# A decoder trunk on one core: attention scores of two pairs in one TensorE group, value products of two pairs together, inverse roots spread by transposes, and a table of holding times in the planner

## The chip, the cores and the metric

The kernel runs on one core of a Trainium2 chip. The metric is device time in microseconds (us) of one execution; three runs of the kernel before gave 423.72, 424.61 and 425.31 us, so the median is 424.61 us. The engines are called as the profile calls them: PE (TensorE's matmuls), PEld (its weight loads, which overlap the matmuls), DVE (VectorE), ACT (ScalarE), POOL (GpSimd) and SP (SyncE, which issues the loads).

## The reference

The program is a two-layer decoder trunk over 256 positions of width 1024. Layer 0 has three head groups that all read one normalized input: sparse attention with three branches (8 query heads in 2 key-value groups), block attention (8 heads) and cross-attention into 256 memory tokens (4 heads). Layer 1 has a retention group and the memory cross-attention again. Each group has a SiLU gate path; the gated outputs go through one output projection and are added to the residual. Cut to what the change touches:

```python
# sparse attention: branches c (compressed blocks), s (selected blocks), w (window)
o_s = einsum(masked_softmax(einsum(q, k_sel) * scale, causal), v_sel)
o_w = einsum(masked_softmax(einsum(q, k_win) * scale, causal), v_win)
o   = gate[0] * o_c + gate[1] * o_s + gate[2] * o_w

# block attention: with 256 positions only the causal own block is left
o = einsum(masked_softmax(einsum(q, k_own) * scale, causal), v_own)

# memory cross-attention, in both layers
o = einsum(softmax(einsum(q, k_mem) * scale), v_mem)

# rms_norm, on x, on the memory and between the layers
y = x * rsqrt(mean(x * x) + eps) * g
```

With 256 positions there are four blocks of 64 to select from and 16 may be taken, so that the selected branch is causal attention over all positions, as the window branch is.

## The kernel before

All activations lie with 256 tokens as two tiles of 128 rows, or turned, with 128 channels in the partitions. A weight arrives as f32 in a `raw` buffer (6 of them), is split into a rounded part `whi` (a cast on ACT) and a rest `wlo` (a subtraction on DVE), with four buffers of each, and three fp32r products (high times high, low times high, high times low) make up one projection in the PSUM banks `bpj`. These projections fill most of PE's time. Between them stand short pieces of plain fp32 work on PE, called groups here, which belong together and aren't interrupted:

- **Score groups** (`pair_scores`, `side_by_side`). Two heads of 64 channels form a pair: one head's operands are in partitions 0 to 63 and the other's in 64 to 127, and their products alternate. They appear in the trace as matmuls of form 64\*128 into the two banks `bs`. A causal pair needs four products (two of 128 columns, two of 256), a memory pair four of 256; the trace has two matmuls for each product.
- **Value groups** (`causal_values`, `mem_attention`). The two heads' outputs go to the two halves of the bank `bo`, in form 128\*64.
- **Transposes** of the weights `p` between softmax and value product, three or four at a time into the one bank `bt`. ACT copies that bank to a `pt` buffer before the next group of transposes may write it. The transposes of rotated queries and keys go to the one bank `btr`.
- **Spreading** (`spread`): three times a column of inverse roots is needed along the free axis; a plain fp32 matmul of the column, broadcast over 128 columns, with the identity does that, into `btr`.

There are eight PSUM banks: three `bpj`, two `bs`, and one each of `btr`, `bt` and `bo`. A pair's softmax is `causal_weights`: DVE adds the mask and takes the maximum, ACT takes the exponential with its sum, DVE the reciprocal, and the scaling is divided between them.

The order on each engine is not that of the code. The class `Plan` records every operation with an estimated price (`price`) and dependencies, and plays a schedule forward (`once`): at each step the engine whose next operation can start first takes it. On PE a group (kind 1: transposes and other plain products, kind 2: score form, kind 3: value form) is not taken the moment its inputs are there, while PE is on fp32r projections (kind 0): it waits until its inputs have been there for `HOLD` = 2000 ns, for every group alike (`order`). `turn` is the estimated price of going from one kind to another, and `arrange` plays 12 rounds with due times from the round before and keeps the best. The order so found is fixed in the program; the engines wait for one another by semaphores. The loads on SP and the order of POOL keep the order of the code.

In the code of layer 0 the sparse pairs 0 to 3 are done one by one (`sparse_pair`), each with a score group for each of two branches and one value group for both; then the memory group with a score and a value group for each of its two pairs; then the block pairs 0 to 3 one by one. In layer 1 the memory group has two score groups and one value group.

Of the kernel before, what the change touches and what calls it, by code (L numbers as in the profile page):

```python
# [16 lines left out]
P = 128  # L17
T = 256
# [31 lines left out]
class Op:  # L50
    __slots__ = ("lane", "calls", "cost", "left", "next", "at", "rank", "kind", "end", "held", "strict", "t", "due", "goal", "spent")


ROUNDS = 12
SLACK = 250
HOLD = 2000
FETCH = 6000
LEAD = 0
RELAX = 3000


class Plan:
# [74 lines left out]
    def add(self, lane, method, args, kw):  # L137
# [29 lines left out]
        step = self.price(lane, method, args, kw, out, reads)  # L167
        op.cost += step
        return op

    def price(self, lane, method, args, kw, out, reads):
        n = out.free_size()
        psum = any(a.tensor.name in self.psum for a in reads)
        if lane == "PE":
            if method == "transpose":
                return 110
            rhs, lhs = args[2], args[1]
            if rhs.dtype == F32R:
                return n / 2.4 + 14
# [44 lines left out]

    def turn(self, mode, kind):
        if mode == kind:
            return 0
        return 95 * (mode > 1 or kind > 1) + (150 if mode > 1 else 50) * (kind == 0)

    def arrange(self):  # L230
        ops = self.ops
        last = {}
        for op in ops:
            op.kind = self.mode(op) if op.lane == "PE" else 0
            op.due = op.rank
            for d in op.left:
                d.next.append((op, True))
            if op.strict or op.lane == "SP":
                if op.lane in last:
                    last[op.lane].next.append((op, False))  # L240
                    op.left.add(("after", last[op.lane]))
                last[op.lane] = op
        best = None
# [29 lines left out]
    def once(self):  # L273
# [8 lines left out]
        while len(done) < len(ops):  # L282
# [22 lines left out]
            if any(c[0] == "dma_start" for c in op.calls):  # L305
# [3 lines left out]
                op.end = dma[0] + 500  # L309
# [11 lines left out]
    def order(self, op, l, now, s, mode):  # L321
        early = max(s, now)
        if l == "PE":
# [6 lines left out]
            return ((0 if s + HOLD < now else 2) if op.kind else 1, 0, op.rank)  # L330
# [10 lines left out]
def trunk(  # L341
# [388 lines left out]
    read = []  # L730

    def pair_scores(q, k, spans):

        s = [bank("s") for _ in range(2)]
        side_by_side([(s[hh][:, a], q[pair_half(hh), tok * P : tok * P + P], k[pair_half(hh), : a.stop - a.start], True, True)
                      for tok, a in enumerate(spans) for hh in range(2)], *read)
        read.clear()
        return [[s[hh][:, a] for a in spans] for hh in range(2)], s

    def causal_weights(ss, gate):  # L740
# [11 lines left out]
        pt = tl("pt", [P, 2, 512], 2)  # L752
# [24 lines left out]
    def mem_attention(eqT, kT, v, szT, y, together):  # L777
        for pr in range(2):
            if pr == 0 or not together:
                o = bank("o")  # L780
                todo, done = [], []
# [4 lines left out]
            _, ss = pair_scores(eqT[:, pr], kT[:, pr], WHOLE)  # L786
# [8 lines left out]
            for hh in range(2):  # L795
                V.reciprocal(sm[:, hh], sm[:, hh])
                for tok in range(2):
# [3 lines left out]
                    else:  # L801
# [3 lines left out]
            c = slice(pr * T, (pr + 1) * T) if together else slice(0, T)  # L805
            todo += [(o[hh * 64 : hh * 64 + 64, c], v[:, kt, (2 * pr + hh) * 64 : (2 * pr + hh + 1) * 64],
                      pt[:, hh, kt * T : (kt + 1) * T], kt == 0 and c.start == 0, kt == 1, *[1] * together) for kt in range(2) for hh in range(2)]
            done.append(got)
            if pr == 0 and together:
                continue  # L810
            side_by_side(todo, *done)
            for i in range(0 if together else pr, pr + 1):
                gated(o[:, i * T : (i + 1) * T] if together else o, szT[:, i], y, i)
# [113 lines left out]
    def sparse_pair(pr):  # L927
        nonlocal kS, vsw, nq, gates, vcR, pcT
        o = bank("o")
        for half in vcR:  # L930
            PE.matmul(o[:, :T], half[:, pr % 2].rearrange("p g f -> p (g f)"), pcT[:, pr // 2], start=half is vcR[0], stop=False)
        todo, done = [], []
        for br in (1, 2):
            pt, got = causal_weights(pair_scores(nq[:, pr], kS[:, br - 1], SPAN)[0],
                                     gates[:, :, br * 8 + 2 * pr : br * 8 + 2 * pr + 2])
            todo += causal_values(pt, lambda g, kt, br=br: vsw[:, kt, (br - 1) * P + g * 64 : (br - 1) * P + g * 64 + 64],
                                  o, False, br == 2)
            done.append(got)
        side_by_side(todo, *done)
        gated(o, szn[:, pr], yn, pr)  # L940
# [47 lines left out]
    def memory_group():  # L988
        nonlocal eqS, szm, memk, memv
        mem_attention(eqS, memk, memv, szm, ym, False)  # L990
# [22 lines left out]
    def block_pairs(*prs):  # L1013
# [6 lines left out]
        for i, pr in enumerate(prs):  # L1020
            pt, got = causal_weights(pair_scores(mq[:, pr], mk[:, pr], SPAN)[0], None)
# [15 lines left out]
    for pr in range(4):  # L1037
        sparse_pair(pr)
# [6 lines left out]
    block_pairs(0)  # L1045
    block_pairs(1)
    block_pairs(2)
    block_pairs(3)

# [87 lines left out]
    mem_attention(eqS1, k1m, v1m, szm1, ym1, True)  # L1137
# [236 lines left out]
```

## Time and profile before

| what | value |
|---|---|
| three runs | 423.72, 424.61, 425.31 us (median 424.61) |
| span of the profiled execution, first to last instruction | 421.8 us; the runs' median is 2.8 us above it |
| PE busy | 415.1 us, 98% of the span, 2320 matmuls |
| DVE busy | 316.4 us, 75% |
| ACT busy | 259.0 us, 61% |
| POOL busy | 10.2 us, 2% |
| granted TensorE clock, mean | 0.998 |
| DMA | 74.20 MB, 176 GB/s on average |

In the timeline a row gives the start and the length of one or more equal instructions in a stretch, both in us, and their count. PE's matmuls are pipelined: the length of one runs into the next, so that what an instruction costs PE is read from start to start. In the view of waits a row says who waited for whom: the total in us, the number of times and the longest. In the view by windows each engine's busy time in a stretch stands beside the number of its instructions. Nearly all operations are recorded by one helper line (337), so that the names of the tiles tell them apart.

### The profile page before, as it was taken

The page shows a single profiled execution, that of the slowest core. Times are in us where ns is not written, and L with a number is a line of the kernel's source. Part 1 is how long each engine was busy: PE and PEld are TensorE (multiplying, and loading weights), DVE is VectorE, ACT ScalarE, POOL GpSimd, SP SyncE. Part 2 cuts the span into 40 slices and gives each one's busy share as a digit, 9 for nine tenths or more (in the row PEclk, how much of TensorE's full clock was granted, in tenths as well). Part 3 has the DMA queues.
Part 4 walks back from the last instruction along what each step waited for, and adds up shares of the span by engine and source line. Part 5 has one row for each costly group of instructions (what it writes and reads, how often), then busy time and mean ns, then how long its engine had stood idle before and what let it go on. Part 6 is the DMA issues. An engine that isn't in the chain of part 4 may idle for free.

```text
span 421.8 us, 6467 instructions
## 1 busy us (share of the span) xinstructions
PE 415.1 (98%) x2320; PEld 344.6 (82%) x2320; DVE 316.4 (75%) x643; ACT 259.0 (61%) x487; POOL 10.2 (2%) x23
## 2 busy tenths in 40 slices
PE   9999999999999999999999999999999999999994
PEld 8988988778878767778887878888888888888884
DVE  3889999999985658647788985865997486564634
ACT  4866648998767558645566745655655455654512
POOL 0000000000000000000000000100100010010001
PEclk9999999999999999999999999999999999999999
DMA  7998844457343392341685544555455555545302
GB/s 228 399 338 265 279 162 141 149 175 253 125 131 120 99 344 76 131 149 50 203 250 197 167 153 149 169 176 194 142 198 180 177 170 172 177 148 186 117 0 99
DMA packets 36975, 74.20 MB, mean 176 GB/s; under 512 B 3024, under 2 KB 22736, under 8 KB 36944
## 3 DMA queue, kind: packets, MB, share of 16 engines
q1 hardware_dynamic: 36512, 73.27, 52.9%
q10 hardware_dynamic: 432, 0.52, 0.4%
q8 instruction: 18, 0.29, 0.3%
q14 instruction: 13, 0.11, 0.1%
HBM read 72.74 MB, written 1.05 MB: 175 GB/s over the span
## 4 chain that ended last, share of the span: by engine, by line
PE 98%; DVE 0%; ACT 0%; issue 0%; POOL 0%; POOLq 0%
PE bpj L337 74%; PE bs L337 10%; PE btr L337 6%; PE bt L337 5%; PE bo L337 4%; ACT p L337 0%; DVE p L337 0%; DVE v L337 0%; DVE rot_b L337 0%; POOL p L337 0%; DVE ss L337 0%; POOL mhalf L337 0%; POOLq L1363 0%
## 5 line engine op out<-in xcount | busy, mean ns | idle before, releaser
L337 DVE TENSOR_TENSOR wlo<-raw,whi 128x1024 fp32r<-128x1024 f32 (+3 forms) x127 | 147.0, 1165 | 56.5 <-ACT whi L337 55.5
L337 ACT CAST whi<-raw 128x1024 fp32r<-128x1024 f32 (+3 forms) x127 | 127.0, 1004 | 80.7 <-PE bpj L337 43.0
L337 PE MATMUL bpj<-whi,big 128*128 128x512 f32 (+1 forms) x496 | 156.0, 387 | 0.0
L337 PEld LDWEIGHTS bpj<-whi,big 128*128 128x128 f32 x496 | 91.8, 188 | 18.7 <-issue 1.3
L337 PE MATMUL bpj<-wlo,big 128*128 128x512 f32 (+1 forms) x248 | 95.8, 386 | 0.0
L337 PE MATMUL bpj<-big,whi 128*128 128x512 f32 (+1 forms) x320 | 79.2, 377 | 0.0
L337 PEld LDWEIGHTS bpj<-big,whi 128*128 128x128 f32 x320 | 53.6, 192 | 7.6 <-issue 0.4
L337 PEld LDWEIGHTS bpj<-wlo,big 128*128 128x128 f32 x248 | 46.6, 188 | 8.8 <-issue 0.3
L337 PE MATMUL bpj<-big,wlo 128*128 128x256 f32 x288 | 46.1, 286 | 0.0
L337 PEld LDWEIGHTS bpj<-big,wlo 128*128 128x128 f32 x288 | 42.2, 190 | 4.7 <-issue 0.7
L337 PE MATMUL bpj<-whi,y 128*128 128x512 f32 x84 | 28.2, 392 | 0.0
L337 ACT COPY pt<-bt 128x384 f32<-128x384 f32 (+1 forms) x32 | 16.2, 505 | 10.3 <-PE bt L337 10.2
L337 ACT ACTIVATE p<-p,mx 128x128 f32<-128x128 f32 (+1 forms) x48 | 21.4, 450 | 1.6 <-DVE mx L337 1.6
L337 PEld LDWEIGHTS bpj<-whi,y 128*128 128x128 f32 x84 | 15.7, 188 | 3.1
L337 ACT COPY rot_a<-bpj 128x256 f32<-128x256 f32 x32 | 11.8, 368 | 9.5 <-PE bpj L337 9.3
L337 PE MATMUL bt<-cst,p 128*128 128x128 f32 x104 | 17.1, 277 | 0.0
L337 PE MATMUL bpj<-wlo,y 128*128 128x512 f32 x42 | 16.6, 396 | 0.0
L337 PEld LDWEIGHTS bt<-cst,p 128*128 128x128 f32 x104 | 12.3, 140 | 4.9 <-issue 2.6
L337 DVE CUSTOM_DVE_ANT_0 p<-bs,cst 128x128 f32<-128x128 f32 (+1 forms) x48 | 14.5, 353 | 1.0 <-PE bs L337 0.8
L337 DVE TENSOR_SCALAR p<-p,sm 128x256 f32<-128x256 f32 (+1 forms) x48 | 14.2, 323 | 1.2
L337 DVE TENSOR_TENSOR rot_a<-bpj,rot_a 128x256 f32<-128x256 f32 x32 | 13.4, 419 | 2.2 <-ACT rot_a L337 2.1
L337 ACT ACTIVATE v<-bpj,rstd 128x512 f32<-128x512 f32 (+1 forms) x18 | 12.4, 689 | 4.0 <-PE bpj L337 2.7
(227 smaller groups left out, 489.7 us busy)
## 6 DMA issues: line engine op xcount, KB each, us to landing
raw<-in_w SPq DMA_DIRECT2D x84, 512.0 KB, 4.4
raw<-in_wout SPq DMA_DIRECT2D x28, 512.0 KB, 3.9
raw<-in_w SPq DMA_DIRECT2D x15, 256.0 KB, 5.8
v<-in_xtok SPq DMA_DIRECT2D x4, 512.0 KB, 7.4
raw<-in_w SPq DMA_DIRECT2D x4, 280.0 KB, 5.0
v<-in_w SPq DMA_DIRECT2D x2, 512.0 KB, 5.4
raw<-in_memT SPq DMA_DIRECT2D x2, 512.0 KB, 4.0
raw<-in_memtok SPq DMA_DIRECT2D x2, 512.0 KB, 3.7
```

Of the source, the lines that this page charges most:

```text
L337: getattr(self.engines[op.lane], method)(*args, **kw)
```

## The change

Four things are changed.

1. **Scores.** `pair_scores` takes one or two pairs. For two pairs, the second one's scores are written to the banks `bo` and `btr`, so that eight products over four banks make up one group. The sparse attention makes one such group for the two branches of each pair (4 groups for 8), the memory group one for its two pairs (1 for 2 in each layer). The block pairs' score groups stay single.
2. **Value products.** `sparse_pairs(0, 1)` and `(2, 3)`, `block_pairs(0, 1)` and `(2, 3)` and the memory group of layer 0 have one value group for two pairs, in the two halves of `bo`, as layer 1 had before. The first pair's weights wait meanwhile in `pt`, the second sparse pair's in two buffers `v4`.
3. **Spreading** is a transpose of the broadcast column in place of a plain fp32 matmul with the identity.
4. **Planner.** In place of one `HOLD` there is a table `HOLDS` with a time for each of the 102 groups, in steps of 500 ns: 18 are 0, 17 are 500 ns, 17 are 1000 ns, and the rest lie between 2 and 20 us. A table `TURNS` replaces the estimated price of a turn, prices of small instructions are raised, a load is taken to land 800 ns later, and there are 5 rounds for 12.

```diff
-ROUNDS = 12
+ROUNDS = 5
 SLACK = 250
-HOLD = 2000
+HOLDS = (
+    8, 16, 0, 1, 1, 6, 40, 4, 16, 2, 6, 16, 0, 6, 2, 1, 4, 2, 16, 8, 6, 12, 6, 16, 40, 4, 0, 8, 16, 16, 8, 2,
...
+)
...
+    TURNS = ((0, 0, 200, 180), (7, 0, 195, 180), (214, 164, 0, 190), (174, 130, 192, 0))
...
+        for op, h in zip(groups, HOLDS):
+            op.hold = 500 * h
...
-            return ((0 if s + HOLD < now else 2) if op.kind else 1, 0, op.rank)
+            return ((0 if s + op.hold < now else 2) if op.kind else 1, 0, op.rank)
...
-            PE.matmul(b[:, tok * P : (tok + 1) * P], col[:, tok : tok + 1].to_broadcast([P, P]), ident,
-                      start=True, stop=True)
+            PE.transpose(b[:, tok * P : (tok + 1) * P], col[:, tok : tok + 1].to_broadcast([P, P]), ident)
...
-    def pair_scores(q, k, spans):
-
-        s = [bank("s") for _ in range(2)]
-        side_by_side([(s[hh][:, a], q[pair_half(hh), tok * P : tok * P + P], k[pair_half(hh), : a.stop - a.start], True, True)
-                      for tok, a in enumerate(spans) for hh in range(2)], *read)
+    def pair_scores(spans, *pairs):
+
+        s = [[bank(t) for t in ("ss", ("o", "tr"))[i]] for i in range(len(pairs))]
+        side_by_side([(s[i][hh][:, a], q[pair_half(hh), tok * P : tok * P + P], k[pair_half(hh), : a.stop - a.start], True, True)
+                      for i, (q, k) in enumerate(pairs) for tok, a in enumerate(spans) for hh in range(2)], *read)
...
+        if second:
+            pt = tl("v4", [P, 2, 512], at=turns[0] % 2 + 6)
+            turns[0] += 1
+        else:
+            pt = tl("pt", [P, 2, 512], 2)
...
-    def sparse_pair(pr):
+    def sparse_pairs(*prs):
+        todo, done = [], []
+        for i, pr in enumerate(prs):
+            both = pair_scores(SPAN, *((nq[:, pr], kS[:, br]) for br in range(2)))
+            for br in (1, 2):
+                pt, got = causal_weights(both[br - 1][0], gates[:, :, br * 8 + 2 * pr : br * 8 + 2 * pr + 2], i)
+                todo.append((i, br, pt))
+                done.append(got)
         o = bank("o")
...
+        side_by_side([x for i, br, pt in todo
+                      for x in causal_values(pt, lambda g, kt: vsw[:, kt, (br - 1) * P + g * 64 : (br - 1) * P + g * 64 + 64],
+                                             o[:, i * T : (i + 1) * T], False, br == 2, True)], *done)
...
-    for pr in range(4):
-        sparse_pair(pr)
+    sparse_pairs(0, 1)
+    sparse_pairs(2, 3)
...
-    block_pairs(0)
-    block_pairs(1)
-    block_pairs(2)
-    block_pairs(3)
+    block_pairs(0, 1)
+    block_pairs(2, 3)
```

The number of PE instructions in the program is the same (2134, of which 6 are now transposes). The order of SP's loads and of POOL's operations is the same; on PE, DVE and ACT the order differs from the first projections on, up to the last 98 instructions of PE. Three places of the instruction order follow. A row has the line of the recording helper (337 before, 349 now), the operation, out<-in by the names of the tiles with their buffer numbers, the size of the result, and the count of equal instructions in a row.

PE before, in the sparse attention: transposes of the weights `p`, one score group of four products on the banks `bs_0` and `bs_1`, and then projections (`bpj`) again.

```order
L337 MATMUL bt_0_69_129<-cst_0_59_119,p_2_3_63 128x128 x3
L337 MATMUL bs_0_67_127<-s2_0_33_93,v4_5_9_69 128x128
L337 MATMUL bs_1_68_128<-s2_0_33_93,v4_5_9_69 128x128
L337 MATMUL bs_0_67_127<-s2_0_33_93,v4_5_9_69 128x256
L337 MATMUL bs_1_68_128<-s2_0_33_93,v4_5_9_69 128x256
L337 MATMUL bpj_2_78_138<-wlo_3_32_92,big_0_12_72 128x512
```

Such a group of four stood eight times in the sparse attention, with a turn into it and out of it each time.

PE now, at the first sparse pair: both branches' scores follow each other.

```order
L349 MATMUL bpj_0_65_125<-big_1_13_73,whi_3_28_88 128x512
L349 MATMUL bs_0_67_127<-s2_0_33_93,v4_5_9_69 128x128
L349 MATMUL bs_1_68_128<-s2_0_33_93,v4_5_9_69 128x128
L349 MATMUL bs_0_67_127<-s2_0_33_93,v4_5_9_69 128x256
L349 MATMUL bs_1_68_128<-s2_0_33_93,v4_5_9_69 128x256
L349 MATMUL bo_0_80_140<-s2_0_33_93,v4_5_9_69 128x128
L349 MATMUL btr_0_72_132<-s2_0_33_93,v4_5_9_69 128x128
L349 MATMUL bo_0_80_140<-s2_0_33_93,v4_5_9_69 128x256
L349 MATMUL btr_0_72_132<-s2_0_33_93,v4_5_9_69 128x256
L349 MATMUL bpj_0_65_125<-big_1_13_73,whi_3_28_88 128x512 x3
```

One group of eight products takes the place of two groups of four, with the banks `bo` and `btr` as the second two.

PE now, in the block attention: two groups of transposes into the one bank `bt`, with output-projection matmuls between them.

```order
L349 MATMUL bt_0_69_129<-cst_0_59_119,p_1_2_62 128x128 x3
L349 MATMUL bpj_1_66_126<-whi_2_27_87,ym_0_16_76 128x512
L349 MATMUL bpj_1_66_126<-wlo_2_31_91,ym_0_16_76 128x512
L349 MATMUL bpj_1_66_126<-whi_2_27_87,ym_0_16_76 128x512
L349 MATMUL btr_0_72_132<-whi_2_27_87,ym_0_16_76 128x512
L349 MATMUL btr_0_72_132<-wlo_2_31_91,ym_0_16_76 128x512
L349 MATMUL bt_0_69_129<-cst_0_59_119,p_2_3_63 128x128 x3
L349 MATMUL btr_0_72_132<-whi_2_27_87,ym_0_16_76 128x512
```

Five matmuls stand between the two groups of transposes here; before, there were mostly twelve or thirteen between two such groups of one block pair.

More of the change, by code (lines that the diff above doesn't have):

```diff
@@ L50 @@
 class Op:
-    __slots__ = ("lane", "calls", "cost", "left", "next", "at", "rank", "kind", "end", "held", "strict", "t", "due", "goal", "spent")
-ROUNDS = 12
+    __slots__ = ("lane", "calls", "cost", "left", "next", "at", "rank", "kind", "end", "held", "strict", "t", "due", "goal", "spent", "hold")
+ROUNDS = 5
 SLACK = 250
-HOLD = 2000
 FETCH = 6000
@@ L167, in add @@
         step = self.price(lane, method, args, kw, out, reads)
+        if lane in ("DVE", "ACT") and out.partition_size() < P:
+            step += 95
         op.cost += step
@@ L242, in arrange @@
                 last[op.lane] = op
+        groups = [op for op in ops if op.lane == "PE" and op.kind]
+        assert len(groups) == len(HOLDS)
+        for op, h in zip(groups, HOLDS):
+            op.hold = 500 * h
         best = None
@@ L308, in once @@
                 dma[0] = s0 + by / (400.0 if t > 5000 else 260.0)
-                op.end = dma[0] + 500
+                op.end = dma[0] + 1300
             else:
@@ L775, in gated, with mem_attention @@
         V.tensor_tensor(y[:, 1, kt], yf, y[:, 0, kt].bitcast(F32), ALU.subtract)
-    def mem_attention(eqT, kT, v, szT, y, together):
+    def mem_attention(eqT, kT, v, szT, y):
+        both = pair_scores(WHOLE, *((eqT[:, pr], kT[:, pr]) for pr in range(2)))
+        todo, done = [], []
         for pr in range(2):
-            if pr == 0 or not together:
-                o = bank("o")
-                todo, done = [], []
             p = tl("p", [P, 2, 512], 3)
@@ L785, in mem_attention @@
             sm = tl("sm", [P, 2, 2], 3)
-            _, ss = pair_scores(eqT[:, pr], kT[:, pr], WHOLE)
+            ss = both[pr][1]
             for hh in range(2):
@@ L804, in mem_attention @@
                                                     for kt in range(2) for tok in range(2)]))
-            c = slice(pr * T, (pr + 1) * T) if together else slice(0, T)
-            todo += [(o[hh * 64 : hh * 64 + 64, c], v[:, kt, (2 * pr + hh) * 64 : (2 * pr + hh + 1) * 64],
-                      pt[:, hh, kt * T : (kt + 1) * T], kt == 0 and c.start == 0, kt == 1, *[1] * together) for kt in range(2) for hh in range(2)]
+            todo.append(pt)
             done.append(got)
[L809 to L813, printed above, removed]
+        o = bank("o")
+        side_by_side([(o[hh * 64 : hh * 64 + 64, pr * T : (pr + 1) * T], v[:, kt, (2 * pr + hh) * 64 : (2 * pr + hh + 1) * 64],
+                       todo[pr][:, hh, kt * T : (kt + 1) * T], kt == 0 and pr == 0, kt == 1, 1)
+                      for pr in range(2) for kt in range(2) for hh in range(2)], *done)
+        for i in range(2):
+            gated(o[:, i * T : (i + 1) * T], szT[:, i], y, i)
     kS = vsw = nq = gates = kcBD = vcR = pcT = eqS = szm = mb = rstdm = rbm = memk = memv = szb = mq = mk = mvt = yb = k1m = v1m = None
@@ L925, in compressed_scores @@
         S.copy(pcT.rearrange("p u t -> p (u t)"), b)
-    def sparse_pair(pr):
-        nonlocal kS, vsw, nq, gates, vcR, pcT
-        o = bank("o")
[L930 to L940, printed above, removed]
+    def sparse_pairs(*prs):
+        todo, done = [], []
+        for i, pr in enumerate(prs):
[4 more added lines that the diff above has]
+                done.append(got)
+        o = bank("o")
+        for i, pr in enumerate(prs):
+            for half in vcR:
+                PE.matmul(o[:, i * T : (i + 1) * T], half[:, pr % 2].rearrange("p g f -> p (g f)"), pcT[:, pr // 2],
+                          start=i == 0 and half is vcR[0], stop=False, skip_group_check=True)
+        side_by_side([x for i, br, pt in todo
+                      for x in causal_values(pt, lambda g, kt: vsw[:, kt, (br - 1) * P + g * 64 : (br - 1) * P + g * 64 + 64],
+                                             o[:, i * T : (i + 1) * T], False, br == 2, True)], *done)
+        for i, pr in enumerate(prs):
+            gated(o[:, i * T : (i + 1) * T], szn[:, pr], yn, pr)
     def memory_queries():
```

21 lines of the change are left out of this document (9 added, 12 removed), and 3 rows, old and new, of the table HOLDS.

## The prediction

> **What bounds the kernel now.** I read the page's span and chain first, then the view of waits for PE, then PE's timeline.
>
> ```profile
> span 421.8 us, 6467 instructions
> PE 98%; DVE 0%; ACT 0%; issue 0%; POOL 0%; POOLq 0%
> ```
>
> ```profile
> PE bt L337 <- POOL mhalf L337: 1.0, 1, 1.0
> ```
>
> The chain that ended last is PE for 98%, and the only wait of PE over the threshold of the view is one of 1.0 us at the very start. So the time is the sum of what PE's instructions cost, and of what goes around it. A wait can't be saved, only PE's work; and any wait that the new order brings is added in full. What a turn from projections to a group and back costs is read from start to start:
>
> ```profile
> 153.88 0.93 PE L337 MATMUL bs<-v,v 64*128 64x128 f32 x8
> 154.73 0.73 PE L337 MATMUL bpj<-whi,big 128*128 128x512 f32 x2
> 155.31 0.39 PE L337 MATMUL bpj<-wlo,big 128*128 128x512 f32 x1
> 155.53 0.63 PE L337 MATMUL bpj<-whi,big 128*128 128x512 f32 x2
> 156.00 0.39 PE L337 MATMUL bpj<-wlo,big 128*128 128x512 f32 x1
> ...
> 156.68 0.39 PE L337 MATMUL bpj<-wlo,big 128*128 128x512 f32 x1
> 157.00 1.08 PE L337 MATMUL bo<-pt,s 128*64 128x256 f32 x8
> 158.01 0.93 PE L337 MATMUL bs<-v,v 64*128 64x128 f32 x8
> 158.87 0.55 PE L337 MATMUL bt<-cst,p 128*128 128x128 f32 x3
> 159.17 0.71 PE L337 MATMUL bpj<-whi,big 128*128 128x512 f32 x2
> ```
>
> Two projection matmuls take 0.47 us (155.53 to 156.00), so one takes about 0.23. The last one ahead of a value group takes 0.32 (156.68 to 157.00): **entering** costs 0.09. The first two after a score group take 0.58 (154.73 to 155.31): **leaving** to projections costs 0.11. A causal score group itself takes 0.85 to 0.86, a memory pair's value group 1.01. The group at 158.01 follows another directly and pays no entry. Leaving to transposes costs less: three take 0.30 (158.87 to 159.17) where they take 0.24 elsewhere:
>
> ```profile
> 90.12 0.49 PE L337 MATMUL bt<-cst,p 128*128 128x128 f32 x3
> 90.36 0.48 PE L337 MATMUL bpj<-whi,big 128*128 128x512 f32 x1
> ```
>
> So 0.06 there. With the matmul behind them a group of three costs about 0.33, or 0.11 for each transpose.
>
> **The change part by part.** *Inside the groups.* What a group of twice the length takes is in the timeline for value groups; the third pair of rows is a memory pair's scores.
>
> ```profile
> 165.66 0.87 PE L337 MATMUL bo<-pt,v 128*64 128x256 f32 x8
> 166.46 0.71 PE L337 MATMUL bs<-v,v 64*128 64x128 f32 x6
> ...
> 93.99 1.52 PE L337 MATMUL bo<-pt,s 128*64 128x256 f32 x16
> 95.44 0.38 PE L337 MATMUL bs<-s,v 64*128 64x128 f32 x2
> ...
> 117.17 1.14 PE L337 MATMUL bs<-s,s 64*128 64x256 f32 x8
> 118.23 0.55 PE L337 MATMUL bt<-cst,p 128*128 128x128 f32 x3
> ...
> 243.96 1.95 PE L337 MATMUL bo<-pt,s 128*64 128x256 f32 x16
> 245.84 0.74 PE L337 MATMUL bpj<-big,whi 128*128 128x512 f32 x2
> ```
>
> Eight causal value matmuls take 0.80 us, sixteen 1.45: the second eight add 0.65. Of memory pairs eight take 1.01 and sixteen 1.88, so 0.87 is added. Two block value groups made one save 2 x 0.80 - 1.45 = 0.15; two sparse ones 2 x 1.45 - (1.45 + 2 x 0.65) = 0.15; the memory pair's 2 x 1.01 - 1.88 = 0.14. That is 2 x 0.15 + 2 x 0.15 + 0.14 = 0.74 us. A score group of two pairs is not in the trace. Its second pair has products of the same sizes, so the value groups' rows are the nearest: 0.65 more for causal ones, 0.87 for memory ones. The other end is a second pair as dear as the first (0.86 and 1.06): no gain inside. I take the former, since both forms show the same cost at a group's two ends: 4 x (2 x 0.86 - 1.51) + 2 x (2 x 1.06 - 1.93) = 0.84 + 0.38 = 1.22 us.
>
> *Between the groups.* Before, there are 16 score and 11 value groups (without the two small ones of the compressed branch, which stay), now 10 and 6. Of the 27, five directly follow another group in the order, of the 16 now two: 22 entries become 14, which saves 8 x 0.09 = 0.72 us. By the order 9 exits before lead to projections and 13 to transposes, 1.77 us; now 8 and 6, 1.24 us. That saves 0.53.
>
> *Spreading.* Two products of the column take four matmuls in the trace:
>
> ```profile
> 27.42 0.61 PE L337 MATMUL btr<-cst,rstd 128*128 128x128 f32 x4
> 27.78 0.48 PE L337 MATMUL bs<-whi,big 128*128 128x512 f32 x1
> ```
>
> They take 0.36 us to the next matmul; two transposes take 0.11 + 0.03 = 0.14 by the rows at 90.12. Three times 0.22 is 0.66 us. If the transpose of a broadcast column needs as much as before, it is nothing; the operands lie as in other transposes, so I take 0.66.
>
> The **sum** of PE's work is 0.74 + 1.22 + 0.72 + 0.53 + 0.66 = 3.87 us. With neither the score joins' nor the spreads' gain it is 1.99. DVE, ACT, POOL and the loads do the same operations as before, so nothing else is saved, and the start and the last 98 PE instructions stand as they did. The span would be 417.9 us; the median lies 2.8 us above the profiled span (424.61 against 421.8), and I keep that distance: 420.7.
>
> *The holding table* costs no PE work, but it removes a cushion. Before, every group was held for 2 us, and a transpose group found the `bt` bank free long ahead:
>
> ```profile
> 130.90 0.49 PE L337 MATMUL bt<-cst,p 128*128 128x128 f32 x3
> ...
> 134.21 0.49 PE L337 MATMUL bt<-cst,p 128*128 128x128 f32 x3
> ```
>
> ```profile
> 103.33 0.49 PE L337 MATMUL bt<-cst,p 128*128 128x128 f32 x3
> 103.92 0.47 ACT L337 COPY pt<-bt 128x384 f32<-128x384 f32 x1
> 104.94 0.49 PE L337 MATMUL bt<-cst,p 128*128 128x128 f32 x3
> ```
>
> The usual distance was 3.3 us (130.90 to 134.21), the shortest 1.61 (103.33 to 104.94). What is needed is 0.59 from the transposes' start to the copy's and 0.47 for the copy, 1.06 us, when ACT is free. In the order shown now, three transposes and five matmuls lie between: 0.33 + 5 x 0.23 = 1.48. By the same count thirteen distances are now under 2 us (four of 1.48, the others 1.57 to 1.98), before only the one of 1.61. PE waits where ACT is in a cast when the transposes end:
>
> ```profile
> L337 ACT CAST whi<-raw 128x1024 fp32r<-128x1024 f32 x114 | 119.3, 1050 | 75.5 <-PE bpj L337 41.1 <-PE btr L337 15.1 <-issue 6.4
> L337 DVE TENSOR_TENSOR wlo<-raw,whi 128x1024 fp32r<-128x1024 f32 x114 | 138.8, 1222 | 53.6 <-ACT whi L337 52.6 <-ACT kcbd L337 0.5
> L337 DVE CUSTOM_DVE_ANT_0 p<-bs,cst 128x128 f32<-128x128 f32 (+1 forms) x48 | 14.5, 353 | 1.0 <-PE bs L337 0.8
> ```
>
> At 1.48 there are 0.42 us to spare, and a cast of 1.05 leaves up to 0.63 to wait. All the thirteen distances together are 21.7 us, so with a whole cast ahead of every copy PE waits 13 x (1.06 + 1.05) - 21.7 = 5.7 us; with none, nothing. A gain is excluded, since PE waits for nothing now. The row at 103.33 had 0.55 to spare and no wait, with ACT nearly full, so I take 0.3 us, near the lower end. The bank `bo` is a second such place: after a double score group its next writers, the compressed branch's products, come some 1.4 us later in the order (three transposes, three matmuls of 512 and two of 256 columns), and DVE has to read two scores from it (2 x 0.353 = 0.71), with a split of 1.22 ahead of them at worst: 0.5 us to wait, at no more than four groups. That lies within the same bounds. The forecast is 420.7 + 0.3 = **421.0 us**.
>
> The Trainium skill (TensorEngine Tiling, "Gotcha 1: PSUM Pressure") says that different row tiles can't use one PSUM bank at the same time, which speaks against the change: a second pair needs two further banks, and this kernel takes them from the value products and the rotations. It gives no price, so the sum by it stays the one above, less a wait at `bo` or `btr`; no row of the kernel before shows four banks so used.
>
> **The rivals.** *First: DVE becomes the bound in the sparse part.*
>
> ```profile
> 70.00:80.00 10.00, 10.00 (x64) 7.89 (x60) 9.71 (x40) 9.66 (x27) 0.00 (x0) 1.00 0.46 143
> 80.00:90.00 10.00, 10.00 (x59) 7.43 (x59) 9.67 (x37) 9.72 (x31) 0.00 (x0) 1.00 0.38 120
> 90.00:100.00 10.00, 10.00 (x71) 8.01 (x70) 9.78 (x29) 8.33 (x19) 0.74 (x1) 1.00 0.83 261
> 100.00:110.00 10.00, 10.00 (x76) 8.22 (x76) 9.59 (x32) 7.73 (x22) 0.00 (x0) 1.00 0.65 212
> 110.00:120.00 10.00, 10.00 (x61) 7.92 (x60) 9.49 (x36) 8.04 (x22) 0.00 (x0) 1.00 0.33 109
> ```
>
> ```profile
> ACT whi L337 <- PE bpj L337: 1.9, 3, 1.0
> ```
>
> DVE (the third pair of numbers) is busy 48.2 of 50 us there and has 1.8 us to give. PE's gain in the sparse part is about 2.2 us: inside the groups 0.84 + 0.30, six groups fewer at about 0.17 less the handovers given up (0.6), two spreads (0.44). If nothing of it can be had, the time is 420.7 + 2.2 = 422.9. Against it: even in this stretch ACT waits three times for PE to free a `whi` buffer, so the splits run ahead of PE by the four buffers, which is far more than 2.2 us of work.
>
> *Second, on the other side: the handovers of `bt` decide.* With a cast ahead of every copy it is 420.7 + 5.7 = 426.4, slower than before; it decides from 3.9 us of such waits on, or 0.3 at each of the thirteen places. Half of it gives 423.6. For it speaks that ACT is busy 9.7 of 10 us in the first two rows above, against it that the copy is shorter than the cast and that four of the distances leave 0.77 us and more. The Trainium skill (TensorE: Matmul & The Clock Gate, "Architectural detail: the array is 16× 32×32, not 1× 128×128", at the engine queue depths) says that ScalarE takes its instructions strictly in order; by that a copy can't pass a cast, and this rival's price holds, without it the waits would be nothing.
>
> *Third: the change doesn't do what it says inside the score groups,* and each pair pays its fill and drain though they share a group: 420.7 + 1.2 = 421.9. For it: no row shows a joined score group. Against it: joined value groups lose that cost in three pairs of rows.
>
> **How the numbers follow.** The forecast has 0.65, the first rival 0.12, the second 0.16 (half of that for the half price, half for the full one or more), the third 0.07. About 0.5%, or 2.1 us, is what a measurement of this kernel tells from no change: faster is below 422.5. The forecast (all but 0.03 of it) and the third rival lie there: 0.69. The first rival and the half of the second are within 0.5%, and so is some of the full price, since 426.4 is 0.4% above: 0.03 + 0.12 + 0.08 + 0.02 = 0.25. Slower is left with 0.06. The range goes from 419.7, if a fifth more is saved than read (0.2 x 3.87 = 0.8) and no wait comes (419.9) with 0.2 for the scatter of a median, to 424.3, which takes in the first rival and the half price (423.6) with most of that scatter above (425.31 - 424.61 = 0.7); the likeliest case alone is 419.9 to 422.0.
>
> **What would show it.** In the profile after, PE's busy share stays at 98% and its waits stay near one of 1.0 us. A causal score group of sixteen takes 1.51 us and a memory one 1.93; a spread of two transposes takes 0.14. The rows of 512 columns keep 0.23 each. `bt` rows that start late, with an idle time of PEld ended by ACT's copy, would show the second rival; `bpj` rows waiting for `wlo` between 70 and 120 us the first. The prediction is wrong if the PE idle time adds up to more than 1.5 us, or if the joined groups' rows sum to the single ones'.

## The result, and the profile after

The changed kernel takes 421.25 us (median of six runs, 420.28 to 423.03) beside 425.1 us of the kernel before: a ratio of 0.9924 with a 95% interval of 0.9901 to 0.9946. The forecast was 421.0 us, in a range of 419.7 to 424.3. A second comparison (e9 below) gave 420.88 us beside 424.13, a ratio of 0.9932 (0.9914 to 0.9950).

The profiled execution has a span of 419.2 us and a time of 421.01 us. Its page, at the head and at the chain that ended last, and its view of waits for PE (who waited for whom, total us, times, longest):

```profile
span 419.2 us, 6447 instructions
PE 94%; DMA 3%; DVE 1%; ACT 1%; SPq 0%; issue 0%
```

```profile
PE bt L349 <- POOL mhalf L349: 1.0, 1, 1.0
PE bpj L349 <- DVE wlo L349: 0.2, 1, 0.2
```

PE is still what the time is made of, and the only wait at `bt` is the old one at the start. The chain's 3% of DMA includes one load of an output weight, 8.10 us on its way, of which more below. What the joined groups cost stands in the timeline for PE (start, length, both in us; what a piece costs is read from start to start):

```profile
26.08 0.38 PE L349 MATMUL btr<-cst,rstd 128*128 128x128 f32 x2
26.21 1.17 PE L349 MATMUL bs<-whi,big 128*128 128x512 f32 x4
...
93.41 0.93 PE L349 MATMUL bs<-s,v 64*128 64x128 f32 x8
94.17 0.27 PE L349 MATMUL bo<-s,v 64*128 64x128 f32 x1
...
94.92 0.73 PE L349 MATMUL bpj<-big,whi 128*128 128x512 f32 x2
...
115.66 1.52 PE L349 MATMUL bo<-pt,s 128*64 128x256 f32 x16
...
118.41 0.50 PE L349 MATMUL bpj<-whi,big 128*128 128x512 f32 x1
...
146.08 1.13 PE L349 MATMUL bs<-s,s 64*128 64x256 f32 x8
...
148.00 0.73 PE L349 MATMUL bpj<-whi,big 128*128 128x512 f32 x2
```

A causal score group of two pairs takes 94.92 - 93.41 = 1.51 us, a memory one 148.00 - 146.08 = 1.92, the sparse value group 118.41 - 115.66 = 2.75, and a spread of two transposes 0.13. The forecast had 1.51, 1.93, 2.75 and 0.14.

The whole of PE's time can be split in this way. The table adds the distances from start to start of all PE rows, from the 131st matmul row (the same projection in both programs, at 23.4 us) to the last matmul. Entries and exits are what the rows at a turn take beyond the same row elsewhere.

| part | forecast, us | before, us | after, us | difference | e9, the same kernel again |
|---|---|---|---|---|---|
| inside score groups | -1.22 | 14.53 | 13.32 | -1.21 | -1.20 |
| inside value groups | -0.74 | 12.92 | 12.16 | -0.76 | -0.76 |
| spreads (by e12) | -0.66 | 1.27 | 0.54 | -0.73 | -0.73 |
| entries, exits, transposes beside them | -1.25 | | | -1.07 | -1.04 |
| projections away from groups | 0 | | | +0.30 | +0.52 |
| single stalls of 0.13 us and more among projections | +0.3 (at `bt`) | 0 | 0.85 | +0.85 | +0.19 |
| sum | -3.57 | 392.38 | 389.77 | -2.61 | -3.02 |

The stalls are not where the forecast had put its 0.3 us. Most of them stand at the first output weights, and the execution of e9 doesn't have them there. The same rows of the two profiles of this kernel, after first and e9 second:

```profile
154.41 0.95 PE L349 MATMUL bpj<-whi,y 128*128 128x512 f32 x2
155.54 0.50 PE L349 MATMUL bpj<-wlo,y 128*128 128x512 f32 x1 [0.18 <-DVE wlo L349]
```

```profile
154.88 0.71 PE L349 MATMUL bpj<-whi,y 128*128 128x512 f32 x2
155.42 0.40 PE L349 MATMUL bpj<-wlo,y 128*128 128x512 f32 x1
```

From the first `whi` product to the first `wlo` product it is 1.13 us in the one and 0.54 in the other. The load of that weight was issued at 145.06 and 145.53 us and landed 8.10 and 7.36 us later. Even in the second its split ended only 0.2 us before PE came to it (155.22 and 155.42 us).

### The profile page after: what moved, and what is told of

The parts are those of the page before. It is cut to its first block, busy times and chain, and to the rows that moved or that the text cites. A ratio compares the mean times of both kernels' runs of the same rounds, so it can differ in the third digit from the quotient of the medians.

```text
span 419.2 us, 6447 instructions
## 1 busy us (share of the span) xinstructions
PE 412.2 (98%) x2314; PEld 343.9 (82%) x2314; DVE 315.8 (75%) x643; ACT 257.8 (62%) x487; POOL 10.5 (2%) x23
## 3 DMA queue, kind: packets, MB, share of 16 engines
HBM read 72.74 MB, written 1.05 MB: 176 GB/s over the span
## 4 chain that ended last, share of the span: by engine, by line
PE 94%; DMA 3%; DVE 1%; ACT 1%; SPq 0%; issue 0%
PE bpj L349 72%; PE bs L349 9%; PE btr L349 5%; PE bo L349 5%; PE bt L349 4%; DMA raw<-in_wout 2%; DMA raw<-in_w 1%; ACT whi L349 0%; SPq L349 0%; DVE wlo L349 0%; DVE yf L349 0%; ACT p L349 0%; DVE p L349 0%; DVE v L349 0%; DVE rot_b L349 0%
## 5 line engine op out<-in xcount | busy, mean ns | idle before, releaser
L349 PE MATMUL bpj<-big,wlo 128*128 128x256 f32 x288 | 45.0, 284 | 0.0
L349 ACT ACTIVATE p<-p,mx 128x256 f32<-128x256 f32 (+1 forms) x48 | 21.5, 452 | 2.3 <-DVE mx L349 2.3
L349 PEld LDWEIGHTS bt<-cst,p 128*128 128x128 f32 x104 | 12.7, 140 | 4.8 <-ACT p L349 1.0
L349 ACT COPY pt<-bt 128x384 f32<-128x384 f32 (+1 forms) x24 | 12.4, 516 | 3.8 <-PE bt L349 3.6
L349 DVE TENSOR_TENSOR v<-bpj,v 128x512 f32<-128x512 f32 x6 | 4.1, 692 | 8.5 <-PE bpj L349 8.5
```

Of the source, the lines that this page charges most:

```text
L349: getattr(self.engines[op.lane], method)(*args, **kw)
```

## The experiments

### The planner without the joins, and one part at a time

Three kernels undo parts of the change and hold every group for 2 us, as the kernel before did. e1 has neither joins nor the new spread, only the new planner:

```diff
-            op.hold = 500 * h
+            op.hold = 2000
-            PE.transpose(b[...], col[...].to_broadcast([P, P]), ident)
+            PE.matmul(b[...], col[...].to_broadcast([P, P]), ident, start=True, stop=True)
-        s = [[bank(t) for t in ("ss", ("o", "tr"))[i]] for i in range(len(pairs))]
+        s = [[bank("s") for t in range(2)] for i in range(len(pairs))]
...
-            both = pair_scores(SPAN, *((nq[:, pr], kS[:, br]) for br in range(2)))
...
-                pt, got = causal_weights(both[br - 1][0], ...
+                pt, got = causal_weights(pair_scores(SPAN, (nq[:, pr], kS[:, br - 1]))[0][0], ...
...
-    sparse_pairs(0, 1)
+    sparse_pairs(0)
+    sparse_pairs(1)
```

> The changed planner alone: scores and value products of each pair in groups of their own again, the spread a matmul again, one holding time of 2 us for every group; the new prices, landing time, turns and number of rounds stay. Theory A (the time is PE's work, and the order only matters where it changes turns): the order has 24 entries into groups, as the kernel before, 8 exits to projections and 16 to transposes against 11 and 13, so 0.16 us less than before: the time of before within 0.5 us, some 425 us. Theory B (the new planner brings the gain): near the changed kernel, 421 to 422 us.

It took 425.98 us beside 423.87 of before, a ratio of 1.0054 (1.0030 to 1.0078). Its waits for PE from 10 us on, of 0.5 us and more:

```profile
PE bpj L348 <- DVE big L348: 0.6, 1, 0.6
PE bpj L348 <- DVE wlo L348: 0.6, 1, 0.6
PE bs L348 <- DVE tmp L348: 0.5, 1, 0.5
```

Its score groups take 14.54 us and its value groups 12.92, the amounts of before; what it takes beyond them is mostly waits. (The profiled execution took 428.01 us, 2.0 us over the median. A further wait of 1.0 us for `whi`, at 7.45 us, isn't of this order: e11 below, in the order of before, has 0.84 us there.) So theory B falls: the planner alone, with 2 us for all, brings nothing. But theory A is only half right: an order with nearly the same turns was 2.1 us slower, because PE waited in it. A table of times for groups that aren't joined was not tried; in the profile of before there is no wait of PE behind the first 1.0 us that it could take away, though it might still save turns.

e2 keeps the joined value groups and the new spread, and has a score group for each pair again (the lines on `bank`, `both` and `pair_scores` of the diff above, the same in the memory group, and 2 us for all).

> The changed kernel with one score group for each pair and branch again, and one holding time of 2 us for every group. Theory A: 1.22 us more inside the groups, and by its order 22 entries for 16 (6 x 0.09 = 0.55) and exits of 2.1 us for 1.44: 2.4 us over the changed kernel, 423.6 us; 423.0 if the wait of 0.7 us for the first output weights goes with the other order. Theory B (joined score groups give nothing inside): 1.2 us over it or less, 422.4 us.

It took 424.53 us, a ratio of 1.0014 (1.0000 to 1.0027). The score groups take 14.53 us again, the value groups 12.16 as in the changed kernel: single score groups cost 1.21 us, which theory B denied. The profile also has 1.3 us of stalls among the projections, enough for the 0.9 us over the 423.6 expected. The longest stands in front of an output projection that waits for the gated output `y`:

```profile
192.42 0.50 PE L348 MATMUL bpj<-whi,y 128*128 128x512 f32 x1 [0.79 <-ACT y L348]
```

e3 undoes the joined value groups.

```diff
-    sparse_pairs(0, 1)
+    sparse_pairs(0)
+    sparse_pairs(1)
...
-    block_pairs(0, 1)
+    block_pairs(0)
+    block_pairs(1)
```

> The changed kernel with one value group for each pair of layer 0 again, and one holding time of 2 us. Theory A: 0.74 us more inside the groups, 19 entries for 16 (0.28) and exits of 1.77 us for 1.44, a little less for transposes: 1.25 us over the changed kernel, 422.5 us. The second pair's weights no longer lie in the buffers that the residual's rows are loaded to, so SP's queue comes to the output weights earlier; if the wait of 0.7 us at the first of them comes from there, it is gone here and the time is 421.8 us. Theory B (value groups were what tied up the bank bo, and joining them gives nothing): 421.2 us.

It took 451.97 us, and it can't be used for the question. The first memory pair's value products are written to the bank `bo` before the second pair's scores have been read from it, so its memory attention in layer 0 is another computation, with other waits; and e4, beside it, shows that the holding time alone costs about 20 us. What single value groups cost is read from e1: 12.92 us for 12.16.

### The table of holding times

e4 is the changed kernel with 2 us for every group, nothing else (the first hunk of e1's diff).

> The changed kernel with one holding time of 2 us for all groups in place of the table. Theory A: the joins do their work in any order; by its order 16 entries, 11 exits to projections and 5 to transposes against 10 and 6, and 49 runs of transposes for 54: the same PE work within 0.1 us, 421.2 us, or 420.5 if the wait of 0.7 us goes. Theory B (the table earns a part of the gain, as its short holding times fit the groups in where they cost least): 422.5 us or more.

It took 442.62 us beside 423.87, a ratio of 1.0444 (1.0419 to 1.0469). Theory A falls. Theory B's "422.5 us or more" holds, but nothing in it led to 20 us. Its waits for PE, the longest:

```profile
PE bt L348 <- ACT v L348: 2.3, 3, 1.2
PE bpj L348 <- ACT y L348: 2.1, 1, 2.1
...
PE bt L348 <- DVE p L348: 1.9, 1, 1.9
```

PE now waits for softmax weights and for the gated outputs (`y`): its order has no projections for it to do meanwhile. How late the chain of groups is shows at the last value group of layer 0, in the timelines for PE of before, after and e4:

```profile
184.84 0.87 PE L337 MATMUL bo<-pt,v 128*64 128x256 f32 x8
```

```profile
185.97 1.52 PE L349 MATMUL bo<-pt,v 128*64 128x256 f32 x16
```

```profile
204.98 1.56 PE L348 MATMUL bo<-pt,v 128*64 128x256 f32 x16
208.65 0.50 PE L348 MATMUL bpj<-whi,y 128*128 128x512 f32 x1 [2.11 <-ACT y L348]
```

The changed kernel's first sparse score group starts at 93.41 us (before at 69.58), and yet the chain ends with that of before. With 2 us for each group it ends 19.0 us later. The 2 us alone don't do it: e2 has them too, with the same joined value groups but single score groups, and took 424.53 us. Its first sparse score group starts at 70.47 us, that of e4 at 102.85. So the holding time costs its 18 us only together with the joined score groups; why these start so late isn't shown.

Two causes were open: the holding itself, and SP's queue. The weights `pt` of the second sparse pair lie in two buffers `v4` into which the residual's rows are loaded afterwards, and the output weights stand behind those rows. In e4 the rows could be loaded at 155.48 us, with no load since 120 us (in the changed kernel at 143.29, after 31 us without a load):

```profile
82.34 38.12 SPq L348 DMA_DIRECT2D raw<-in_w  x20
155.48 0.98 SPq L348 DMA_DIRECT2D v<-in_xtok  x2
...
157.26 18.15 SPq L348 DMA_DIRECT2D raw<-in_wout  x10
```

e5 holds every group 0.5 us, e6 holds 2 us and loads the rows later:

```diff
-            op.hold = 500 * h
+            op.hold = 500
```

> The changed kernel with one holding time of 0.5 us for all groups in place of the table; e4 with 2 us for all took 442.6 us. Theory C (a joined pair is a longer chain of groups; 2 us of holding at each group of it makes the chain so long that PE runs out of projections that it may do meanwhile): with 0.5 us the chain is short again, 421 to 422.5 us; by the order 12 exits to projections and 4 to transposes against 10 and 6, 0.1 us more. Theory D (SP's queue: the residual's rows wait for a buffer of the second sparse pair, and the output weights behind them): the queue stands as in e4, 430 us or more. Theory E (only times for each group, as in the table, make an order without waits): 428 us or more.

```diff
-            op.hold = 500 * h
+            op.hold = 2000
-    x0 = [load(tl("v4", [P, D], at=6 + tok), xtok[:, tok]) for tok in range(2)]
-    g1 = load(tl("v4", [P, D], at=4), grow[0:1].to_broadcast([P, D]))
+    x0 = [tl("v4", [P, D], at=6 + tok) for tok in range(2)]
+    g1 = tl("v4", [P, D], at=4)
...
+                if not last and i == 3 and u == 0:
+                    for tok in range(2):
+                        load(x0[tok], xtok[:, tok])
+                    load(g1, grow[0:1].to_broadcast([P, D]))
```

> As e4, one holding time of 2 us, and the loads of the residual's rows and gain stand behind six loads of output weights in the code, so that these don't wait for a buffer of the second sparse pair. Theory C: the chain of groups is as long as in e4, PE still runs out of what it may do: 432 to 443 us. Theory D: 421 to 424 us.

e5 took 422.85 us beside 423.91, a ratio of 0.9974 (0.9964 to 0.9984); e6 took 429.92, 1.0150 (1.0130 to 1.0171). The last value group of layer 0 in e5 and in e6:

```profile
184.33 1.52 PE L348 MATMUL bo<-pt,v 128*64 128x256 f32 x16
```

```profile
194.76 1.56 PE L348 MATMUL bo<-pt,v 128*64 128x256 f32 x16
198.43 0.50 PE L348 MATMUL bpj<-whi,y 128*128 128x512 f32 x1 [2.11 <-ACT y L348]
```

With a short holding time the chain ends at 184.33 though SP's queue stands as it was, so theory D can't be the whole, and theory E falls in its strong form: one time for all groups is 20 us better than another. Theory C is borne out by e5, but e6 lies between its 432 to 443 us and theory D's 421 to 424: with the rows out of the way, 2 us of holding still cost 6 us over before, and 12.7 us less than in e4. So with joined score groups the holding delays PE by itself too. The planner of e6 also made another order, so how much of the 12.7 us belongs to the queue alone isn't settled.

e5 has the same group times as the changed kernel (13.32 and 12.16 us) and still takes 1.6 to 2 us more. Its largest wait shows one thing that a table can do better than one short time (the profile is of the slowest of its ten runs, 423.96 us):

```profile
27.36 0.43 PE L348 MATMUL btr<-cst,rstd 128*128 128x128 f32 x2 [1.38 <-POOL rstd L348]
```

Taken 0.5 us after it was due by the planner's estimate, the spread came 1.38 us before POOL had finished the root.

### The rows' place in SP's queue

e7 has the changed kernel's table, and the same order on PE, DVE and ACT. Only SP's three loads move.

```diff
     def play(self):
-        for op in self.arrange():
+        todo = self.arrange()
+        late = [op for op in todo if op.calls[0][1][0] in self.late]   # x0[0], x0[1], g1
...
+        todo = [op for op in todo if op not in late]
+        k = todo.index(at) + 1                                         # at: the sixth load of wout
+        todo[k:k] = late
+        for op in todo:
```

> The changed kernel with its table and the same order on PE, DVE and ACT; on SP alone the three loads of the residual's rows and gain go behind the sixth load of output weights. In the changed kernel's trace the first output weight was issued at 145.1 us, right behind those rows, landed at 153.2, and PE stood 0.7 us for its split at 154.9. If SP's queue is the cause, the weight lands before 140 us, that wait is gone and the time is 0.7 us less: 420.5 us. If the split was late for ACT or DVE's sake, the wait and the time stay: 421.2 us.

It took 420.55 us beside 423.91, a ratio of 0.9932 (0.9918 to 0.9945). The output weights were loaded from 116 us on, and the stall at 154.9 us was gone:

```profile
116.19 25.28 SPq L361 DMA_DIRECT2D raw<-in_wout  x6
```

That looked like the 0.7 us gained. But the median of before was lower too in this comparison, and the ratio was no better than the first. So both ran again on one chip:

> The changed kernel itself, to stand beside e10 on the same chip. Theories A and C as well as the trace of the first run: 421.2 us, with a wait of 0.7 us at the first output weights near 155 us; in e7 and e8, of the same order on PE, the matmul at 42.4 us came 0.4 us late, which the changed kernel's first profile doesn't have: if that is chance, it shows in one of two profiles here, and no difference follows from it.

> The kernel of e7 again. If the move of three loads is worth the wait that it took away (0.70 us in the profiles), the median lies 0.5 to 0.9 us under that of e9, and the ratio to before is 0.0017 lower; if another wait (at 42.4 us) takes its place, it is within 0.3 us of e9.

e9 (the changed kernel) took 420.88 us and e10 421.15, both a ratio of 0.9932 to before (0.9914 to 0.9950, and 0.9917 to 0.9946). The move is worth nothing that these runs can tell, and e9 doesn't have the stall either. It isn't a single accident, though: e8 below, with the same order on PE and on SP, has 1.04 us between the same two products where e9 has 0.54, and its load was on the way for 8.00 us. So the changed order leaves that weight so little time that the landing decides, which differs from one execution to the next; in the order of before PE comes to the first of these products at 163.63 us, 14 us after the weight's landing. The wait at 42.4 us isn't of the move: against the first profile, e7 is 0.5 us late there, e9 0.3, e10 0.8, and e8, without the move, waits there for 0.21 us where e7 waits for 0.23.

### The cushion at the bank `bt`

e8 keeps the changed kernel's order and does ACT's copy out of `bt` twice; e11 does the same to the kernel before in its own order.

```diff
+    def twice(self, op):
+        op.calls.append(op.calls[0])
+        return op
...
-            got = S.copy(pt[:, hh, :384], transposes([...]))
+            got = plan.twice(S.copy(pt[:, hh, :384], transposes([...])))
```

> The changed kernel in the same order, with ACT's copy of each bank of transposed weights done twice (24 copies of 0.47 to 0.57 us more), so that the bank bt comes free that much later. In the changed kernel's trace no transpose waits for it; the copy ends at least 0.14 us ahead, then 0.28 and 0.32, at six places 0.42 to 0.44. Theory A (the handovers have cover): the waits are 0.43 + 0.3 + 0.25 + 6 x 0.05, 1.3 us, and up to as much again where ACT comes late to other work: 422.5 to 423.8 us. Theory F (the handovers decide, each of the thirteen short ones waits): 13 x 0.47 = 6.1 us, 427.4 us.

> The kernel before in its own order, with ACT's copy of each bank of transposed weights done twice, as in e8. Between the end of ACT's copy and the next transposes into bt its trace has 0.55 us once, 1.07 once and 2.0 or more at 20 places; the changed kernel's has 0.20 to 0.8 at fifteen. Theory G (the new order spent the cushion at bt, and that is why e8 cost 8.3 us): no more than 0.5 us, 424 to 424.6 us. Theory H (12 us more work on ACT costs that much in any order, since splits come late): 427 us or more.

e8 took 429.56 us, 1.0137 of before (1.0123 to 1.0151): 8.3 us more than the changed kernel in the first comparison. e11 took 424.65 beside 424.13, 1.0020 (1.0009 to 1.0031). The waits for PE at `bt`, in e8 and in e11:

```profile
PE bt L353 <- ACT pt L353: 3.3, 8, 0.6
PE bt L353 <- ACT v L353: 2.3, 3, 1.1
```

```profile
PE bt L341 <- ACT pt L341: 0.3, 1, 0.3
```

Theory G holds: the new order spent the cushion, and the same second copies (32 of them, with those of the memory pairs; the expectation had counted 24) cost 0.5 us in the old order and some 8 in the new one. Theory A's price for e8 was wrong by a factor of three or more, theory F's 6.1 us was nearer and too low as well, and one place shows why. The changed kernel, and then e8, at the same instructions:

```profile
109.92 1.06 ACT L349 CAST whi<-raw 128x1024 fp32r<-128x1024 f32 x1
110.86 0.49 PE L349 MATMUL bt<-cst,p 128*128 128x128 f32 x3
110.88 0.50 ACT L349 ACTIVATE p<-p,sm 128x256 f32<-128x256 f32 x1
111.39 0.48 ACT L349 COPY v<-bt 128x384 f32<-128x384 f32 x1
112.35 0.49 PE L349 MATMUL bt<-cst,p 128*128 128x128 f32 x3
```

```profile
112.21 0.49 PE L353 MATMUL bt<-cst,p 128*128 128x128 f32 x3
112.58 1.06 ACT L353 CAST whi<-raw 128x1024 fp32r<-128x1024 f32 x1
113.53 0.52 ACT L353 ACTIVATE p<-p,sm 128x256 f32<-128x256 f32 x1
113.94 0.98 ACT L353 COPY v<-bt 128x384 f32<-128x384 f32 x2
114.98 0.55 PE L353 MATMUL bt<-cst,p 128*128 128x128 f32 x3 [1.11 <-ACT v L353]
```

In both, a cast and a scaling stand ahead of the copy on ACT. In the changed kernel the cast began 0.94 us before the transposes, so the copy came 0.53 us after their start and the bank was free 0.48 us before it was needed. In e8 ACT was behind by its earlier second copies and began the cast 0.37 us after the transposes; the copy came 1.73 us after their start and was done twice, and the next transposes started 2.77 us after the last for 1.49. ACT keeps its order, so that work added to one copy moves into the next handover.

### The spread alone

e12 is the kernel before in its own order on all engines, with transposes for the spreads (the planner keeps the old price for them).

```diff
-            PE.matmul(b[...], col[...].to_broadcast([P, P]), ident, start=True, stop=True)
+            PE.transpose(b[...], col[...].to_broadcast([P, P]), ident)
```

> The kernel before in its own order on all engines, with the spread of the inverse roots as transposes: that part of the change alone. By the rows of before and of the changed kernel a spread takes 0.36 us as a matmul and 0.135 as a transpose: three times 0.226, 0.68 us less, 423.2 to 423.4 us beside 423.9 of before, and PE's own time from the first to the last matmul 0.68 us less, if nothing waits in its place. A rival: the two spreads that don't stand right before projections gain nothing, as what follows them waits for the spread row: 0.2 us less.

It took 423.49 us beside 424.13, a ratio of 0.9991 (0.9978 to 1.0004). The interval holds no change too, so the time alone doesn't decide; the rows do:

```profile
27.75 0.38 PE L337 MATMUL btr<-cst,rstd 128*128 128x128 f32 x2
27.88 0.48 PE L337 MATMUL bs<-whi,big 128*128 128x512 f32 x1
```

The spread takes 0.13 us for 0.36, all three together 0.54 for 1.27, and PE's time from the 131st row to the last falls from 392.38 to 391.65 us, by the same 0.73. Nothing waited in its place, so the rival falls.

## Why the prediction was right, and where it was not

**What bounds it.** Right: PE's busy share stayed at 98% and the medians fell by 3.85 and 3.25 us in two comparisons, where 3.6 was forecast. That 421.25 lies within 0.25 us of 421.0 is in part luck: PE's own time fell by 2.61 and 3.02 us in the profiles where the sum had 3.57, and the median of before moved between 423.87 and 425.1 us from one comparison to the next.

**Inside the groups.** 1.96 us forecast, 1.97 measured. The step that had no row, the joined score groups, was taken from the value groups' rows and came out to 0.01 us. The third rival (no gain inside) falls by the rows at 93.41 and 146.08, and by e2.

**Spreading.** 0.66 forecast, 0.73 measured: the transposes before other transposes gained a little more.

**Between the groups.** 1.25 forecast, 1.05 measured. The counts and prices of entries and exits were right: by the rows the entries cost 0.71 us less (0.72 forecast) and the exits 0.52 (0.53). What is missing stands beside transposes; the new order has more runs of them among the projections (54 for 51), which the sum left out, but that they explain it isn't shown. The projections away from groups took 0.3 to 0.5 us more, which the forecast put at nothing. In e12, with the order of before, they didn't. What makes them dearer stays open.

**The distance from span to median.** The forecast kept 2.8 us. The runs of the changed kernel have 1.8 between span and time in each execution (421.01 - 419.2), so the profiled execution of before lay about 1.0 us under its own median. That didn't move the forecast, since the same distance was added to both.

**The holding table** is the step that was only half right. "It removes a cushion" was right: e8 and e11 show it at 8 us against 0.5. The wait of 0.3 us at `bt` that it was to cost did not come; the second rival's mechanism is real, and it stood some tenths of a microsecond off. But the step named only what the table takes. Joined pairs with the old 2 us need 442.6 us (e4): with the old time for all groups the change loses 18.7 us instead of gaining. e5 shows that one short time for all gets most of the gain back (422.85 us). The forecast had the built order and its counts, and so its number didn't suffer from that; as an account of what the parts of the change are for, it was wrong.

**The bank `bo` and DVE.** No wait of PE at `bo` or `btr`, and none for `wlo` between 70 and 120 us, shows in the changed kernel's waits, so neither the first rival nor the use of four banks had a price here. The Trainium skill (TensorEngine Tiling, "Gotcha 1: PSUM Pressure") has different row tiles write to different PSUM banks and gives no price. The score groups do that, and by the rows four banks cost PE nothing inside the group: 1.51 us is what the rows of the value groups, with one bank, had led to.

**Left out.** The forecast said that the order of SP's loads is the same. It is, but the residual's rows now wait for another buffer, and all output weights queue behind them. Before, they queued there too, behind the gain's row: no load was issued for 17 us, and the first output weight at 142.99 us. In the changed kernel it was 31 us, and the first one at 145.06, while the order on PE asks for that weight about 9 us earlier. That cost 0.6 us in one profile and nothing in the next; in e4 no load was issued for 35 us.

## What to carry to other kernels

Here one engine set the end, and the sum of what its instructions cost from start to start came out within 0.02 us inside the groups, also for a form that no row showed, because its ends and its inside could be read from other rows. A planner's parameter that costs no work can still be worth more than the work saved: where pieces are joined, it has to be asked whether the old value would still do. And a small difference that one profile shows at one place should be looked for in other profiles of the same order before it is mended.

## What the runs showed of the hardware that was not expected

A wait of PE can cost more than itself. In e4 the granted clock fell three times behind waits, and each time for 3.41 us. All changes of the clock in this trace lie multiples of 3.41 us apart, as if time were cut into stretches of that length. e4 by such stretches, before and after two of the three falls (behind the length stand the busy time and the count of PE, PEld, DVE, ACT and POOL, then the granted clock and two figures of the DMA):

```profile
134.47:137.88 3.41, 1.74 (x14) 1.19 (x16) 2.92 (x18) 3.31 (x14) 0.00 (x0) 1.00 0.01 2
137.88:141.29 3.41, 3.41 (x18) 2.48 (x15) 2.88 (x19) 1.80 (x6) 0.00 (x0) 0.50 0.00 0
...
206.15:209.56 3.41, 1.30 (x10) 0.91 (x7) 2.88 (x6) 1.16 (x3) 0.00 (x0) 1.00 0.49 144
209.56:212.97 3.41, 3.41 (x10) 2.64 (x9) 1.39 (x2) 0.72 (x2) 0.00 (x0) 0.50 0.51 163
```

```profile
210.23 0.63 PE L348 MATMUL bpj<-wlo,y 128*128 128x512 f32 x1
210.66 0.63 PE L348 MATMUL bpj<-whi,y 128*128 128x512 f32 x1
```

After the wait of 2.11 us before 208.65 PE worked for 0.9 us at full speed. Then the granted clock fell to a half, and seven projections took 0.43 us each from start to start instead of 0.23: 1.4 us more. In e6 a wait of the same 2.11 us (before 198.43) was followed by a clock of 1.00. Its stretches, counted in the same steps from the clock's first change in that trace, cut the wait in two:

```profile
193.69:197.10 3.41, 2.62 (x23) 1.83 (x21) 1.95 (x2) 2.47 (x3) 0.00 (x0) 1.00 0.02 6
197.10:200.52 3.42, 2.10 (x9) 1.75 (x10) 2.10 (x6) 0.74 (x2) 0.00 (x0) 1.00 0.73 217
```

So in these two traces it isn't the length of one wait that decides but the idle time within a stretch: 1.67 us and more (3.41 less 1.74) came before each fall, 1.32 us and less (3.42 less 2.10) before none. The view's busy times rest on modelled ends of matmuls, so these two figures are estimates. The Trainium skill (TensorE: Matmul & The Clock Gate, "Part 1: The HAM clock gate (the "warmup" mystery)") says that the clock is halved after at least one idle window of about 3.4 us, and that the windows run freely and don't start anew with a kernel. The steps of 3.41 us and half the clock agree with these traces; but no window was idle throughout here, and about half of one sufficed.
